# Two-layer diffusion trunk in fp32: the second gate's buffer placed elsewhere, the last grouped head's gate product and low part on VectorE, its context sums in a score bank

## The chip, the cores and the metric

The kernel runs on one core of a Trainium2 chip. The metric is the device time of one execution in microseconds (us). The engines are named as in the profile: PE (TensorE), DVE (VectorE), ACT (ScalarE), POOL (GpSimd), SP (SyncE, which issues nearly all DMAs here). Everything is float32. A matrix product in this precision is done as three fp32r matmuls: each operand is split into a high part (a cast to fp32r) and a low part (the rest), and high x high, low x high and high x low are added up in one PSUM bank.

## What is computed

Two layers of a trunk with two attention branches. Layer 0 has 512 latent and 256 context tokens (768 in all), layer 1 only the 512 latent ones are carried on. Per layer, cut to what matters:

```
hx, hc = adaLN-modulated RMSNorm of x (512 x 1024) and ctx (256 x 1024)
px = hx @ w_in                     # q, k, v of both branches, gate paths a_z, b_z, merge gates g_a, g_b
a_att = neighbourhood attention    # 8 heads of 64, 8 x 16 windows, also reads all context keys
b_att = grouped-query attention    # 8 query heads of 64, 2 key/value heads, reads all 768 keys
o_a = (a_att * silu(a_z)) @ w_o_a
o_b = (b_att * silu(b_z)) @ w_o_b
x   = x + gate_x * ((sigmoid(g_a) * o_a + sigmoid(g_b) * o_b) @ w_out)
# layer 0 does the same for the context tokens, which read context keys only
```

Layer 0 is called L0 below, layer 1 L1 (line numbers are written L352 and so on, with three or four digits).

## The kernel before

The program is one long Python function per layer, and a scheduler that simulates a timeline decides in which order each engine gets its instructions. Each engine then works its own list strictly in that order and waits on semaphores.

The grouped attention of a layer (`pipeline` with `gq_first` and `gq_values`) goes through the eight heads with one head of lag: the scores of head h, then the values of head h-1. In between PE gets filler work, here the product with `w_o_a` (tiles `gah`, `gal` for the high and low part of branch a's gated result, PSUM tile `psf`, written with `evac_a`, L593). A head's values are made in six steps. In each, PE transposes four 128x128 blocks of probabilities into a `pst` bank (L670), ACT casts them to the high part `pth` (L673), DVE subtracts for the low part `ptl` (L674), and PE multiplies both with the values into a `psv` bank (L973, L974). There are two `pst` banks. After the sixth step `head_out` adds the two halves of `psv` (ACT copy L682, DVE add L683, both in the single tile `ho`) and multiplies the sum into the gated tile `zb` (POOL, L684); the next copy into `ho` waits until that product has been read. In L0 each head also has context queries: one more step, whose sums have 256 columns and go to the same `psv` bank (`ctx_values`, L747 and L748), and a second `head_out`.

Before the last head's values, `early` allocates the buffers of the next stage and fills three quarters of `gated["b"]`. This is the split of `zb` into `gbh` (ACT cast, L558) and `gbl` (POOL subtraction, L559) by `hilo`, one instruction each per quarter f. The last quarter, f=3, needs the last two heads and is split after the pipeline. Then comes the product with `w_o_b` in four chunks (`o_chunks`), evacuated by `evac_b` (DVE L1008 and L1009, ACT L1011, DVE L1012) against the merge gate tiles `tg`. `load_tg` (L562) brings one from DRAM; `tg[1]` serves output columns f=0 to 3, `tg[3]` columns f=4 to 7. The filler product with `w_o_b`, once branch a's is done, goes to `psf`; after the pipeline five banks named `psx` are opened over those that the scores (`pss`, two of two banks each) and values (`psv`, one) had.

`big(name)` hands out large SBUF buffers from one pool in rotation. A tile that gets a buffer waits until the last reader of the tile that had it before is done. By the buffers of the program before, in L0 `tg[3]` lies where the queries `qb` were, `gbh` where the staged keys `gk` were and `gbl` where `gal` was. In L1 the three lie behind `qb`, `gal` and `gah`.

Of the kernel before, what the change touches and what calls it, by code (L numbers as in the profile page):

```python
# [12 lines left out]
ALU = mybir.AluOpType  # L13
# [55 lines left out]
def hybrid_kernel(es: ExitStack, tc, x, ctx, cvec, w_ada, w_ada0, small, gvec, w_in, w_o_a, w_o_b, w_out,  # L69
# [421 lines left out]
    def layer(l, hx, nxt, mid):  # L491
# [60 lines left out]
        def hilo_tiles(name):  # L552
            return [big(name + part).rearrange("p (f n) -> p f n", f=4) for part in "hl"]

        def hilo(src, dst, fs):
            sv = src.rearrange("p (f n) -> p f n", f=4)
            for f in fs:
                S.copy(R(dst[0][:, f, :ntok]), sv[:, f, :ntok])  # L558
                G.tensor_tensor(R(dst[1][:, f, :ntok]), sv[:, f, :ntok], dst[0][:, f, :ntok], ALU.subtract)  # L559

        def load_tg(c):
            nc.sync.dma_start(tg[c].rearrange("p (f n) -> p f n", f=4)[:, :, :ntok], gs[c][:, :, :ntok])  # L562
# [88 lines left out]
        if True:  # L651
# [25 lines left out]
            def head_out(po, e, dst):  # L677

                n = dst.shape[-1]
                m, o = 64 * e, 64 * (1 - e)  # L680
                t1 = att["p"].tile([128, 512], F32, tag="ho", name=nm("ho"), bufs=1)
                S.copy(t1[m:m + 64, :n], po[o:o + 64, :n])  # L682
                V.tensor_tensor(t1[m:m + 64, :n], po[m:m + 64, :n], t1[m:m + 64, :n], ALU.add)  # L683
                G.tensor_tensor(dst, dst, t1[m:m + 64, :n], ALU.mult)  # L684

            def rows(a, half):
                return a[64 * half:64 * half + 64]
# [53 lines left out]
            def ctx_values(p, vsl, dst, e):  # L741
                hi, lo = transpose_split(
                    [(p[:, 256 * i + 128 * k:256 * i + 128 * k + 128], 256 * k + 128 * i)
                     for k in range(2) for i in range(2)])
                po = psw(256, "v")
                for k in range(2):
                    T.matmul(po, vsl(4 + k), hi[:, 256 * k:256 * k + 256], start=k == 0, stop=False)  # L747
                    T.matmul(po, vsl(4 + k), lo[:, 256 * k:256 * k + 256], start=False, stop=k == 1)  # L748
                head_out(po, e, dst)
# [88 lines left out]
            def pipeline(fill, spread, scores_of, values_of, last=None, bg=[]):  # L838

                n = len(fill)  # L840
                prev = None
                for h in range(8):
                    att["bg"] = bg if h > 3 or pm["n"] == 1 else []
                    st = scores_of(h)
                    if prev is not None:
                        values_of(h - 1, prev)
                    run(fill, len(fill) - (n - n * min(h + 1, spread) // spread))
                    prev = st
                if last is not None:
                    run(fill, len(fill))  # L850
                    last()
                run(bg, len(bg))
                values_of(7, prev)
                run(fill, len(fill))

            akt = [k_tile(e, True) for e in range(2)]

            def na_first(h):
                j, e = h // 2, h % 2
# [124 lines left out]

            def early():

                for c in (1, 3):
                    tg[c] = big("tg")
                    load_tg(c)
                gated["b"] = hilo_tiles("gb")  # L990
                hilo(zb, gated["b"], range(3))
            bg = gate_steps((1,), att["p"]) if first else []
# [3 lines left out]
        with tc.tile_pool(name=f"mrg{l}", bufs=1, reuse_waits="tile") as mp:  # L996
            open_ps(x=5)
            extra = lambda name: mp.tile([128, 3072], F32, tag="extra", name=nm(name))
            gv = mp.tile([128, nv, DM], F32, tag="gate", name=nm("gate"), bufs=1)
            for v in range(nv):  # L1000
                src = gd[l][8 * v:8 * v + 8].rearrange("k p -> (k p)").unsqueeze(0)
                nc.sync.dma_start(gv[:, v, :], src.to_broadcast([128, DM]))
            hilo(zb, gated["b"], [3])
            mg = []

            def evac_b(f, n0, n1, ps):
                a, b = tg_part(0, f, n0, n1), tg_part(1, f, n0, n1)
                V.scalar_tensor_tensor(b, b, 1.0, ps, ALU.add, ALU.mult)  # L1008
                V.tensor_tensor(a, a, b, ALU.add)  # L1009
                hi, lo = [m[:, f % 4, n0:n1] for m in mg[f // 4]]  # L1010
                S.copy(R(hi), a)  # L1011
                V.tensor_tensor(R(lo), a, hi, ALU.subtract)  # L1012
            chunks = o_chunks("b", None, evac_b)
            chunks[0][0]()
            for i in range(4):
                if i < 3:
                    chunks[i + 1][0]()
                if i % 2 == 0:
                    mg.append(hilo_tiles("m"))
                for piece in chunks[i][1]:  # L1020
                    piece()

            nt = 6 if first else 4
            xv = [a.rearrange("p (t n) -> p t n", t=3) for a in (big("xt0"), extra("xt1"))]
            xts = []
            for t in range(nt):
                xt = xv[t // 3][:, t % 3, :]
                nc.sync.dma_start(xt, x_src(t) if first else xs1[128 * t:128 * t + 128, :])
                xts.append(xt)
            a_m = lambda part, k: mg[k // 4][part][:, k % 4, :]  # L1030
            bg = ada_steps(1, range(16), (1,), 2, mp) + [lambda: ada_mod(1)] if first else []
            run(bg, 1)
            per_bg = -(-len(bg) // nt)
            for n in range(2):
                w = load_w(w_out[l], 512 * n, 512, KT, mix_lo)

                def evac_o(t, ps, n=n, c=(0, 512)):
                    cs = slice(512 * n + c[0], 512 * n + c[1])
                    t1 = mp.tile([128, 512], F32, tag="t1", name=nm("t1"), bufs=2)[:, :c[1] - c[0]]
                    V.tensor_tensor(t1, ps, gv[:, 0 if t < 4 else 1, cs], ALU.mult)  # L1040
                    xt = xts[t]
                    V.tensor_tensor(xt[:, cs], xt[:, cs], t1, ALU.add)
                    if not first:
                        nc.sync.dma_start(o_lat[16 * t:16 * t + 16][:, :, cs], xt[:, cs])
                    elif n == 1:
                        if t < 4:
                            nc.sync.dma_start(xs1[128 * t:128 * t + 128, :], xt)
                        late.append(lambda: make_hx(1, t, xt, nxt(), mp))
                late = []
                for t in range(nt):  # L1050
                    if not first and n == 1 and t == nt - 1:
                        for c in ((0, 256), (256, 512)):
                            ps = psw(256)
                            tok_mm(ps, [[a[:, c[0]:c[1]] for a in x] for x in w], 256, a_m, t, 0, KT)
                            evac_o(t, ps, c=c)
                        break
                    tok_proj(w, 512, a_m, t, evac_o)
                    run(bg, per_bg)
                    run(late, len(late) - 1)
                run(late, len(late))  # L1060
# [186 lines left out]
```

## Time and profile before

| what | value |
|---|---|
| runs | 1146.18, 1144.71, 1144.48 us; median 1144.71 |
| profiled execution | 1144.91 us, of which 1143.1 us span from the first to the last instruction |
| granted PE clock | 0.999 |
| instructions | 17425, of which PE 6128 matmuls and as many weight loads |
| DMA | 135.08 MB, mean 118 GB/s |

The profiled execution is 0.20 us above the median. PE is busy nearly throughout: of the 40 slices of the span its row shows 9 tenths or more in all but the first and the last. The stages that the change touches are the ends of the grouped attention, at about 490 to 575 us (L0) and 1027 to 1090 us (L1). A row of the timeline reads: start, duration, engine, line, operation, tile written, tiles read, sizes, and in brackets the engine's idle time just before with the instruction that ended it.

### The profile page before, as it was taken

What the parts mean: (1) busy time and instruction counts of PE and PEld (TensorE: products, weight loads), DVE (VectorE), ACT (ScalarE), POOL (GpSimd) and SP (SyncE); (2) the same over time, 40 slices, a digit from 0 to 9 for tenths busy, and PEclk for the clock granted to TensorE, in tenths of its full rate; (3) what the DMA queues carried; (4) which work ended last, traced back from release to release, by engine and by line L of the source; (5) the groups of instructions that cost most, each with busy time, mean ns of one, the idle gap of its engine ahead of it and who ended that gap; (6) DMA issues with size and microseconds to landing.
All of it is one profiled execution on the core that took longest, in us unless ns stands there. A gap on an engine that the chain in (4) does not pass through costs nothing.

```text
span 1143.1 us, 17425 instructions
## 1 busy us (share of the span) xinstructions
PE 1120.7 (98%) x6128; PEld 947.6 (83%) x6128; DVE 816.3 (71%) x1535; ACT 581.4 (51%) x1185; POOL 480.6 (42%) x449
## 2 busy tenths in 40 slices
PE   7999999999999999999999999999999999999998
PEld 5788888888988888888788787888887888887787
DVE  6777688887554786697588655469777665898573
ACT  6553366665443565666330355337666355766521
POOL 1073354553364333453511226345453664465311
PEclk9999999999999999999999999999999999999999
DMA  9645212333323232451434424633332333152133
GB/s 368 241 123 157 85 56 70 99 116 97 118 94 97 96 101 86 98 217 38 152 124 134 148 69 122 186 103 116 99 114 65 111 103 102 65 175 92 64 126 97
DMA packets 91886, 135.08 MB, mean 118 GB/s; under 512 B 10804, under 2 KB 55064, under 8 KB 91160
## 3 DMA queue, kind: packets, MB, share of 16 engines
q1 hardware_dynamic: 91520, 133.87, 36.9%
q8 instruction: 48, 0.79, 0.3%
q14 instruction: 38, 0.31, 0.1%
q10 hardware_dynamic: 280, 0.12, 0.0%
HBM read 116.63 MB, written 17.32 MB: 117 GB/s over the span
## 4 chain that ended last, share of the span: by engine, by line
PE 87%; DVE 5%; DMA 2%; ACT 2%; issue 2%; POOL 1%; SPq 0%; ACTq 0%; POOLq 0%; DVEq 0%
PE psx L352 12%; PE psx L354 12%; PE psx L353 12%; PE psf L352 10%; PE psf L353 10%; PE psf L354 10%; PE pst L670 5%; PE pss L792 3%; PE pss L719 2%; PE pss L720 2%; PE psv L974 2%; PE psv L973 1%; PE pst L432 1%; DVE ptl L674 1%; DMA rawb<-in_w_ada_dram 1%
## 5 line engine op out<-in xcount | busy, mean ns | idle before, releaser
L674 DVE TENSOR_TENSOR ptl<-pst,pth 128x512 fp32r<-128x512 f32 (+1 forms) x176 | 115.9, 671 | 43.4 <-ACT pth L673 42.4
L673 ACT CAST pth<-pst 128x512 fp32r<-128x512 f32 (+1 forms) x176 | 99.2, 577 | 93.2 <-PE pst L670 53.1
L352 PE MATMUL psf<-hx,whi 128*128 128x512 f32 (+1 forms) x368 | 140.1, 381 | 0.1
L339 POOL TENSOR_TENSOR wlo<-raw,whi 128x512 fp32r<-128x512 f32 x68 | 95.9, 1414 | 103.5 <-ACT whi L337 86.2
L353 PE MATMUL psf<-hx,whi 128*128 128x512 f32 (+1 forms) x368 | 138.0, 375 | 0.0
L354 PE MATMUL psf<-hx,wlo 128*128 128x512 f32 (+1 forms) x368 | 137.6, 374 | 0.0
L352 PE MATMUL psx<-whi,hx 128*128 128x512 f32 (+1 forms) x368 | 137.6, 375 | 0.0
L354 PE MATMUL psx<-whi,hx 128*128 128x512 f32 (+1 forms) x368 | 135.8, 369 | 0.0
L353 PE MATMUL psx<-wlo,hx 128*128 128x512 f32 (+1 forms) x368 | 135.7, 369 | 0.0
L337 ACT CAST whi<-raw 128x512 fp32r<-128x512 f32 x136 | 82.8, 620 | 51.3 <-DMA raw<-in_w_in_dram 32.5
L322 ACT CAST whi<-raw 128x512 fp32r<-128x512 f32 x88 | 53.9, 622 | 100.5 <-PE psx L354 38.3
L670 PE MATMUL pst<-ident,p 128*128 128x128 f32 x640 | 99.5, 272 | 1.4 <-DVE ptl L674 0.9
L325 POOL TENSOR_TENSOR wlo<-raw,whi 128x512 fp32r<-128x512 f32 x36 | 49.5, 1378 | 119.6 <-ACT whi L322 106.2
L339 DVE TENSOR_TENSOR wlo<-raw,whi 128x512 fp32r<-128x512 f32 x68 | 68.0, 1001 | 32.1 <-ACT whi L337 31.6
L670 PEld LDWEIGHTS pst<-ident,p 128*128 128x128 f32 x640 | 77.8, 141 | 13.4 <-DVE ptl L674 1.3
L660 POOL TENSOR_TENSOR p<-p,r 128x512 f32<-128x512 f32 (+1 forms) x64 | 83.5, 1305 | 4.9
L659 POOL TENSOR_SCALAR r<-r 128x1 f32<-128x1 f32 x64 | 22.2, 347 | 150.4 <-DVE r L654 126.9
L352 PEld LDWEIGHTS psx<-whi,hx 128*128 128x128 f32 x368 | 69.5, 189 | 12.3 <-issue 0.8
L354 PEld LDWEIGHTS psx<-whi,hx 128*128 128x128 f32 x368 | 69.4, 189 | 11.9
L354 PEld LDWEIGHTS psf<-hx,wlo 128*128 128x128 f32 x368 | 69.3, 188 | 11.7
L353 PEld LDWEIGHTS psx<-wlo,hx 128*128 128x128 f32 x368 | 69.5, 189 | 10.7
L352 PEld LDWEIGHTS psf<-hx,whi 128*128 128x128 f32 x368 | 69.4, 189 | 10.5 <-ACT zt L517 0.3
(253 smaller groups left out, 3049.7 us busy)
## 6 DMA issues: line engine op xcount, KB each, us to landing
raw<-in_w_in_dram SPq DMA_DIRECT2D x168, 256.0 KB, 2.9
rawb<-in_w_ada_dram SPq DMA_DIRECT2D x64, 256.0 KB, 2.8
gs<-zt SPq DMA_DIRECT2D x32, 256.0 KB, 2.0
raw<-in_w_out_dram SPq DMA_DIRECT2D x32, 256.0 KB, 2.9
tg<-gs SPq DMA_DIRECT2D x4, 1536.0 KB, 6.8
rawx<-in_w_ada_dram SPq DMA_DIRECT2D x8, 512.0 KB, 7.7
raw<-in_w_o_a_dram SPq DMA_DIRECT2D x16, 256.0 KB, 2.7
raw<-in_w_o_b_dram SPq DMA_DIRECT2D x16, 256.0 KB, 3.3
```

The costliest lines, as they stand in the source:

```text
L322: S.copy(hi[:, :n], raw[:, :n])
L325: e.tensor_tensor(lo[:, :n], raw[:, :n], F(hi[:, :n]), ALU.subtract)
L337: S.copy(hi, raw)
L339: lo_eng(i).tensor_tensor(lo, raw, F(hi), ALU.subtract)
L352: T.matmul(ps, lhs[0], rhs[0], start=first, stop=False)
L353: T.matmul(ps, lhs[0], rhs[1], start=False, stop=False)
L354: T.matmul(ps, lhs[1], rhs[0], start=False, stop=last)
L660: G.tensor_tensor(p[:, c0:c1], p[:, c0:c1], r[:, i:i + 1].to_broadcast([128, c1 - c0]), ALU.mult)
L670: T.transpose(pt[:, c0:c0 + 128], src, ident)
L673: S.copy(hi[:, n0:n1], pt[:, n0:n1])
L674: V.tensor_tensor(lo[:, n0:n1], pt[:, n0:n1], F(hi[:, n0:n1]), ALU.subtract)
L792: T.matmul(pss.rearrange("p (a b n) -> p a b n", a=2, b=2), qi, blocks_of(k, *at), start=b, stop=not b)
```

## The change

It has four parts. `tg[3]` is no longer allocated and loaded in `early`, but in the loop over the chunks of `o_b`, behind the load of the second chunk's weights. So `gbh` and `gbl` move up one place in the rotation. In L0 `gbh` now lies behind `qb`, `gbl` behind `gk` and `tg[3]` behind `gal`; in L1 they lie behind `qb`, `gal` and `gah`. A flag `att["end"]` is set before the values of the last grouped head: with it `head_out` multiplies on DVE instead of POOL, and `ctx_values` takes its bank from the scores (`"s"`) instead of the values (`"v"`). The split of the last quarter f=3 is done span by span (512 columns, in L0 also 256), its low part on DVE.

```diff
-        def hilo(src, dst, fs):
+        def hilo(src, dst, fs, parts=None, lo=G):
             sv = src.rearrange("p (f n) -> p f n", f=4)
             for f in fs:
-                S.copy(R(dst[0][:, f, :ntok]), sv[:, f, :ntok])
-                G.tensor_tensor(R(dst[1][:, f, :ntok]), sv[:, f, :ntok], dst[0][:, f, :ntok], ALU.subtract)
+                for a, b in parts or [(0, ntok)]:
+                    S.copy(R(dst[0][:, f, a:b]), sv[:, f, a:b])
+                    lo.tensor_tensor(R(dst[1][:, f, a:b]), sv[:, f, a:b], dst[0][:, f, a:b], ALU.subtract)
...
-                G.tensor_tensor(dst, dst, t1[m:m + 64, :n], ALU.mult)
+                (V if att["end"] else G).tensor_tensor(dst, dst, t1[m:m + 64, :n], ALU.mult)
...
-                po = psw(256, "v")
+                po = psw(256, "s" if att["end"] else "v")
...
                 run(bg, len(bg))
+                att["end"] = last is not None
                 values_of(7, prev)
...
-                for c in (1, 3):
-                    tg[c] = big("tg")
-                    load_tg(c)
+                tg[1] = big("tg")
+                load_tg(1)
                 gated["b"] = hilo_tiles("gb")
                 hilo(zb, gated["b"], range(3))
...
-            hilo(zb, gated["b"], [3])
+            hilo(zb, gated["b"], [3], spans, V)
...
             for i in range(4):
                 if i < 3:
                     chunks[i + 1][0]()
+                if i == 0:
+                    tg[3] = big("tg")
+                    load_tg(3)
```

How the order moves, at three places. In the rows below, numbers behind a name tell tiles apart.

The end of L0's last head on PE, before: `psf` is the first product with `w_o_b`, `psv_6333` the head's values, `psv_6413` its context sums and `psx_6479` the first tile of the next stage.

```order
L670 MATMUL pst_6404<-ident,p_6155 128x128 x4
L974 MATMUL psv_6333<-ptl_6395,vb_3516 128x512
L353 MATMUL psf_6462<-gbl_6326,whi_6438 128x512
L354 MATMUL psf_6462<-gbh_6325,wlo_6440 128x512
L352 MATMUL psf_6462<-gbh_6325,whi_6444 128x512
L353 MATMUL psf_6462<-gbl_6326,whi_6444 128x512
L354 MATMUL psf_6462<-gbh_6325,wlo_6446 128x512
L747 MATMUL psv_6413<-pth_6409,vb_3516 128x256
L748 MATMUL psv_6413<-ptl_6410,vb_3516 128x256
```

And the same place in the changed program.

```order
L353 MATMUL psf_6464<-gbl_6324,whi_6444 128x512
L354 MATMUL psf_6464<-gbh_6323,wlo_6446 128x512
L976 MATMUL psv_6331<-pth_6381,vb_3516 128x512
L977 MATMUL psv_6331<-ptl_6382,vb_3516 128x512
L976 MATMUL psv_6331<-pth_6392,vb_3516 128x512
L671 MATMUL pst_6402<-ident,p_6155 128x128 x4
L977 MATMUL psv_6331<-ptl_6393,vb_3516 128x512
L748 MATMUL pss_6411<-pth_6407,vb_3516 128x256
L749 MATMUL pss_6411<-ptl_6408,vb_3516 128x256
```

All nine matmuls of `psf` with quarters f=0 to 2 now stand in a row ahead of the head's last values (before, they were spread over these, the last five behind the transposes of the context step), so nothing stands between the last transposes and the context sums, which go to a `pss` bank. Behind the context sums `psx` begins in both programs. Its first tile lies in the bank of `pss_6411` now and waits for the DVE sum that reads that; before, its first tile lay in a free score bank, and the second one, in the bank of `psv_6413`, waited for that sum.

The same stretch of L0 on DVE, before:

```order
L674 TENSOR_TENSOR ptl_6410<-pst_6404,pth_6409 128x512
L683 TENSOR_TENSOR ho_6400<-psv_6333,ho_6400 64x512
L683 TENSOR_TENSOR ho_6418<-psv_6413,ho_6418 64x256
L1008 SCALAR_TENSOR_TENSOR tg_6321<-tg_6321,psf_6462 128x512
L1008 SCALAR_TENSOR_TENSOR tg_6321<-tg_6321,psx_6479 128x256
```

And changed:

```order
L675 TENSOR_TENSOR ptl_6408<-pst_6402,pth_6407 128x512
L684 TENSOR_TENSOR ho_6398<-psv_6331,ho_6398 64x512
L685 TENSOR_TENSOR zb_4170<-zb_4170,ho_6398 64x512
L684 TENSOR_TENSOR ho_6416<-pss_6411,ho_6416 64x256
L685 TENSOR_TENSOR zb_4170<-zb_4170,ho_6416 64x256
L560 TENSOR_TENSOR gbl_6324<-zb_4170,gbh_6323 128x512
L560 TENSOR_TENSOR gbl_6324<-zb_4170,gbh_6323 128x256
```

The two products `zb` and the low part of f=3 have come over from POOL. On POOL the low parts of f=0 to 2 have moved up as well: two of them from behind the last product with `gal` to right behind a `zb` of the sixth head, ahead of a softmax division `p`, the third behind that division.

L1 on PE, before, where five of the six matmuls of `psf` that use f=0 and 1 stand (the sixth, `gbh` x `whi`, stands some twelve rows ahead of them):

```order
L670 MATMUL pst_11528<-ident,p_11300 128x128
L353 MATMUL psf_11871<-gbl_11754,whi_11847 128x512
L354 MATMUL psf_11871<-gbh_11753,wlo_11849 128x512
L352 MATMUL psf_11871<-gbh_11753,whi_11847 128x512
L973 MATMUL psv_11472<-pth_11522,vb_9709 128x512
L353 MATMUL psf_11871<-gbl_11754,whi_11847 128x512
L354 MATMUL psf_11871<-gbh_11753,wlo_11849 128x512
L974 MATMUL psv_11472<-ptl_11523,vb_9709 128x512
```

And changed:

```order
L352 MATMUL psf_11873<-gbh_11753,whi_11847 128x512
L353 MATMUL psf_11873<-gbl_11754,whi_11847 128x512
L354 MATMUL psf_11873<-gbh_11753,wlo_11849 128x512
L352 MATMUL psf_11873<-gbh_11753,whi_11847 128x512
L976 MATMUL psv_11474<-pth_11502,vb_9711 128x512
L353 MATMUL psf_11873<-gbl_11754,whi_11847 128x512
L354 MATMUL psf_11873<-gbh_11753,wlo_11849 128x512
L977 MATMUL psv_11474<-ptl_11503,vb_9711 128x512
```

The five have moved up two steps of the head's values, to the wait for `ptl_11503` (`ptl_11501` before). Around this place in L1, POOL now has the two low parts ahead of a weight's low part `wlo` and a division `p`, and DVE has a `wlo` ahead of the score maximum `mx` instead of behind it.

The DMA of `tg[3]` moves on SP's queue from among the weights of `w_o_b` to behind the first weight of `w_out`; behind it now stand further weights of `w_out`, the gate `gv` and the residual tiles.

More of the change, by code (lines that the diff above doesn't have):

```diff
@@ L856, in layer @@
             akt = [k_tile(e, True) for e in range(2)]
+            att["end"], att["turn"] = False, 0
             def na_first(h):
```

## The prediction, made before the changed kernel ran

> **What bounds the kernel now.** I read the page's busy times first, then the chain that ended last, then the waits in the two stretches that the change touches, then the timelines of PE, ACT, DVE and POOL there. On the page:
>
> ```profile
> PE 1120.7 (98%) x6128; PEld 947.6 (83%) x6128; DVE 816.3 (71%) x1535; ACT 581.4 (51%) x1185; POOL 480.6 (42%) x449
> PE 87%; DVE 5%; DMA 2%; ACT 2%; issue 2%; POOL 1%; SPq 0%; ACTq 0%; POOLq 0%; DVEq 0%
> tg<-gs SPq DMA_DIRECT2D x4, 1536.0 KB, 6.8
> ```
>
> PE is busy for 1120.7 of 1143.1 us and is 87% of the chain. The change takes no matmul away. So all it can win is the 22.4 us in which PE does nothing, start and end of the program included, and of these only the waits that it touches. A faster DVE, ACT or POOL gains nothing except where PE waits for it. The longest two waits of L0's stretch, 549 to 561 us, are not PE's own (total, count, longest):
>
> ```profile
> POOL gbl L559 <- PE psf L353: 3.6, 1, 3.6
> ACT ho L682 <- POOL zb L684: 3.1, 1, 3.1
> ```
>
> `gbl` could not start before PE had read its buffer for the last time, and the copy `ho` waited for the product `zb`, which stood behind it on POOL. PE's timeline shows, in brackets, what came of both: 0.79 us of idle time put down to `gbl` and 1.21 us put down to the DVE add `ho`.
>
> ```profile
> 552.43 0.48 PE L352 MATMUL psf<-gbh,whi 128*128 128x512 f32 x1
> ...
> 554.43 0.60 PE L670 MATMUL pst<-ident,p 128*128 128x128 f32 x4
> 554.78 0.48 PE L974 MATMUL psv<-ptl,vb 128*128 128x512 f32 x1
> 555.10 0.40 PE L353 MATMUL psf<-gbl,whi 128*128 128x512 f32 x1
> ...
> 555.57 0.40 PE L352 MATMUL psf<-gbh,whi 128*128 128x512 f32 x1
> 556.75 0.50 PE L353 MATMUL psf<-gbl,whi 128*128 128x512 f32 x1 [0.79 <-POOL gbl L559]
> ...
> 557.79 0.28 PE L352 MATMUL psx<-gbh,whi 128*128 128x256 f32 x1
> ...
> 558.74 0.28 PE L354 MATMUL psx<-gbh,wlo 128*128 128x256 f32 x1
> 560.22 0.50 PE L352 MATMUL psx<-gbh,whi 128*128 128x512 f32 x1 [1.21 <-DVE ho L683]
> ```
>
> Starts give the pace: 0.23 us for a matmul of 512 columns (two steps from 555.10 to 555.57), 0.32 behind transposes (554.78 to 555.10), 0.35 for four transposes (554.43 to 554.78), and 0.12 for 256 columns (557.79 to 558.74 are eight steps). By that pace 556.75 is 0.95 late and 560.22 is 1.36 late: 2.3 us of stall in L0. The other engines:
>
> ```profile
> 555.07 0.59 ACT L673 CAST pth<-pst 128x512 fp32r<-128x512 f32 x1 [1.76 <-PE pst L670]
> 555.68 0.58 ACT L682 COPY ho<-psv 64x512 f32<-64x512 f32 x1
> 559.34 0.36 ACT L682 COPY ho<-psv 64x256 f32<-64x256 f32 x1 [3.09 <-POOL zb L684]
> ...
> 551.43 1.78 DVE L339 TENSOR_TENSOR wlo<-raw,whi 128x512 fp32r<-128x512 f32 x1
> 555.69 0.69 DVE L674 TENSOR_TENSOR ptl<-pst,pth 128x512 fp32r<-128x512 f32 x1 [1.28 <-ACT pth L673]
> 556.41 0.69 DVE L683 TENSOR_TENSOR ho<-psv,ho 64x512 f32<-64x512 f32 x1
> 559.74 0.43 DVE L683 TENSOR_TENSOR ho<-psv,ho 64x256 f32<-64x256 f32 x1 [2.64 <-ACT ho L682]
> 568.10 0.68 DVE L325 TENSOR_TENSOR wlo<-raw,whi 128x512 fp32r<-128x512 f32 x1
> 574.13 0.42 DVE L1008 SCALAR_TENSOR_TENSOR tg<-tg,psx 128x256 f32<-128x256 f32 x1
> ...
> 550.82 5.87 POOL L559 TENSOR_TENSOR gbl<-zb,gbh 128x768 fp32r<-128x768 f32 x3 [3.60 <-PE psf L353]
> 558.03 1.28 POOL L684 TENSOR_TENSOR zb<-zb,ho 64x512 f32<-64x512 f32 x1
> ```
>
> **L0, step by step.** The low parts of f=0 to 2 move up on POOL to right behind the sixth head's `zb`, when PE has done the last scores that read `gk`; `gbl` then waits for nothing that PE is about to use, and the 0.95 goes. PE runs its nine `psf` matmuls from 552.43 without a stop (0.32 and eight times 0.23, to 554.59), then three value matmuls (to 555.28), then the context step's transposes. The cast `pth` starts 0.64 behind them (555.07 against 554.43), at 555.92; `ptl` 0.62 behind that (555.69 against 555.07), at 556.54; the 512-column `ho` add 0.72 later (556.41 against 555.69), at 557.26, done 557.95.
>
> Now `zb` on DVE. No row shows it. The nearest are the add of the same shape, 0.69, and a DVE subtraction with both inputs in SBUF, 0.68 at 568.10 and 1.78 at 551.43. In the second POOL had begun its first `gbl` (1.9 of 5.87) 0.6 us before, and 551.43 + 1.78 is some 0.5 us behind that one's end: DVE was held until POOL had finished an instruction. I take 0.68, because in the new order POOL has nothing of the old cluster left at this time; 1.78 is the upper end. So `zb` ends at 558.65, the 256-column copy starts at 558.68, the add 0.40 later (559.74 against 559.34), at 559.08, and PE follows 0.48 after that (560.22 against 559.74), at 559.56.
>
> The catch is which matmul that is. Before, the nine 256-column matmuls of the first `psx` ran ahead of the wait, in a free score bank. Now they are the ones that wait, since the context sums lie in the bank that they get. They take 1.07 us (0.95 for eight steps, and 0.12), so the 512-column `psx` starts at 560.63 instead of 560.22: **L0 loses 0.4 us**. The 2.3 us of old stall go, but PE now waits where work used to lie between the context step's transposes and its values (about 0.6 for `pth` and 0.6 for `ptl`) and some 1.9 us in front of `psx` (`ptl` is done at 557.23, and the last of the four context matmuls starts 0.4 later). Bounds: -2.3 (no wait left) and +1.5 (with 1.1 more for `zb`).
>
> The Trainium skill, page "SBUF — State Buffer", section "Who interferes with whom", has a rule against this part: a DVE instruction with two SBUF inputs shares a read port with POOL, and whichever starts first holds it for its whole instruction. The row with 1.78 agrees. By that rule alone, with any POOL work in front of `zb`, the sum for L0 would be +1.5 instead of +0.4.
>
> The low part of f=3 on DVE (0.69 by the same row) and `zb` with 256 columns follow behind the add, from 559.5 on, and end by about 561.5, casts included; PE has `psx` matmuls of f=0 to 2 before it, 1.07 and nine at 0.23, to 562.7. That cover makes them free; without it the 1.1 us of two DVE instructions would be PE's. The `tg[3]` DMA now waits for the last product with `gal`, the same event that released `gbl` at 550.82, and takes 6.8: it lands near 557.6. Its first reader comes behind the evacuations of f=3, the last of which is at 574.13. That is 16 us of cover. What stands around it on SP's queue:
>
> ```profile
> 538.65 19.65 SPq L320 DMA_DIRECT2D raw<-in_w_out_dram  x3
> ```
>
> These three weights went out over 538.65 to 558.30, one by one as buffers came free; a `tg[3]` at 550.8 stands behind the first of them and holds the other two up only until a moment at which the queue was still waiting for buffers. I put the move at 0, with 0.3 either way.
>
> **L1.** PE, then DVE, then POOL:
>
> ```profile
> 1053.34 0.48 PE L352 MATMUL psf<-gbh,whi 128*128 128x512 f32 x1
> ...
> 1055.62 0.50 PE L974 MATMUL psv<-ptl,vb 128*128 128x512 f32 x1 [1.54 <-DVE ptl L674]
> 1057.21 0.48 PE L353 MATMUL psf<-gbl,whi 128*128 128x512 f32 x1
> 1058.93 0.60 PE L670 MATMUL pst<-ident,p 128*128 128x128 f32 x4
> 1060.93 0.65 PE L670 MATMUL pst<-ident,p 128*128 128x128 f32 x4 [0.43 <-DVE ptl L674]
> 1074.70 0.50 PE L974 MATMUL psv<-ptl,vb 128*128 128x512 f32 x1 [0.23 <-DVE ptl L674]
> ...
> 1052.34 0.95 DVE L956 TENSOR_REDUCE mx<-pss 128x1 f32<-128x768 f32 x1
> 1053.21 1.75 DVE L339 TENSOR_TENSOR wlo<-raw,whi 128x512 fp32r<-128x512 f32 x1
> 1054.88 1.27 DVE L674 TENSOR_TENSOR ptl<-pst,pth 128x512 fp32r<-128x512 f32 x2
> ...
> 1051.56 1.42 POOL L339 TENSOR_TENSOR wlo<-raw,whi 128x512 fp32r<-128x512 f32 x1 [0.30 <-PE pst L670]
> 1054.38 2.95 POOL L559 TENSOR_TENSOR gbl<-zb,gbh 128x512 fp32r<-128x512 f32 x2
> ```
>
> PE waits 1.54 us for a `ptl` that DVE starts at 1054.88, because `wlo` in front of it ended only at 1054.96 (1.75 in place of 0.68), 0.58 behind the moment at which POOL went over from one instruction to the next, 1054.38: it was held by what POOL did before. In the new order `wlo` starts in the slot of `mx`, at 1052.34, is held only until POOL's first `gbl` ends (about 1052.7, an estimate: half of 2.95 from 1051.26, when POOL was idle), and `mx` follows it; `ptl` starts near 1054.05, 0.8 earlier. Meanwhile PE has the five `psf` matmuls to do, 1.15 us at 0.23, so the matmul with `ptl` starts at about 1055.05, 0.6 earlier than 1055.62. The five are then missing in 1057.21 to 1058.47, where only `ptl` binds, so the transposes at 1058.93 come 1.1 us earlier. From there to 1074.70 the two `pst` banks set the pace (the wait at 1060.93 is such a one): transposes, cast, subtraction, in a loop that PE cannot speed up. What reached it early stays early: **L1 gains 1.1 us**. Bounds: 0, if the loop is bound by something else ahead of it, and -1.8, the two waits 1.54 and 0.23 whole. POOL's `p` behind the two low parts comes 2.5 us later; it belongs to the eighth head, and the transposes at 1058.93 are still the seventh's, so that costs nothing. At L1's end the products on DVE touch a stretch in which PE has the `psx` matmuls of f=0 to 2 to do, without a wait: 0.
>
> The casts `gbh`, moved up by tens of us on ACT, cost nothing if they slip between casts that PE needs; the slow rival is about that. All other shifts of order lie where PE's timeline shows no wait: 0, with 0.3 either way.
>
> **Sum.** +0.4 - 1.1 = -0.7 against the profiled execution, 1144.91, which is 0.2 above the median shown: **1144.2 us**. Its own bounds: from -2.3 - 1.8 to +1.5 + 0, so 1140.8 to 1146.4; a measurement of this kernel cannot tell changes under about 0.2%, or 2.3 us.
>
> **Rivals.** *All stalls go.* If the bank of the context sums came free before PE gets to `psx`, or the first `psx` got another bank, L0 would gain its 2.3 and L1 up to 1.8: 1140.8. For it: the nine `psf` matmuls in a row give DVE a free field. Against it: 1.9 us separate the last context matmul from the add that frees the bank, and nothing in PE's order fills them.
>
> *The low part in L1 stays late.* `gbl` still lies behind `gal` there, whose last reader on PE stands right ahead of that of `gah`. If it then comes no earlier than before, PE's five moved matmuls wait for it, L1 gains nothing and only L0's loss is left: 1145.3.
>
> *DVE held by POOL.* If a POOL weight split starts just ahead of `zb`, the 1.1 us of the bounds come on top: 1145.3 again with L1's gain, decided by whether POOL is at work at about 558. That is the rule of the Trainium skill's page above ("SBUF — State Buffer", "Who interferes with whom") at this place.
>
> *Slower: a cast blocks ACT.* In L0 the cast of `gbh` for f=1 now stands right ahead of two `pth` casts and waits for a `zb` of POOL:
>
> ```profile
> 497.80 0.84 POOL L684 TENSOR_TENSOR zb<-zb,ho 64x256 f32<-64x256 f32 x1 [1.81 <-DVE ho L683]
> 498.24 1.07 ACT L673 CAST pth<-pst 128x512 fp32r<-128x512 f32 x2 [3.69 <-PE psv L973]
> 500.29 1.28 DVE L674 TENSOR_TENSOR ptl<-pst,pth 128x512 fp32r<-128x512 f32 x2
> ```
>
> `zb` ends at 498.64 and the cast takes some 0.8 (half again the 0.54 of a 512-column one in 498.24's row), so the first `pth` is done at 500.0, 0.3 before DVE takes it; what slack PE has beyond that I do not count. If `zb` slips behind two more POOL instructions of 1.28, the casts come 2.6 late and PE loses 2.3; the same at one cast of L1 makes 4.6, and with the sum 1148.8. It decides from 0.3 us of slip. Against it: POOL was idle for 1.81 us ahead of this `zb`, waiting for DVE.
>
> **How the numbers follow.** My forecast 0.58; all stalls go 0.13; L1's low part late 0.12; DVE held 0.09; ACT blocked 0.08. Faster by over 0.2% (below 1142.4) takes the first rival and a tail of 0.05 of the forecast, 0.18 in all; slower (above 1147.0) is the ACT case, 0.08; within 0.2% is the rest, 0.74. The range goes up to the sum's own upper bound and down to where most of L0's and L1's stalls would be won together; it leaves out the end of the first rival and the last one, less than 0.2: 1141.7 to 1146.4.
>
> **What would show it.** In the changed profile: no wait of `psf` on `gbl` in L0; POOL's first `gbl` long before 549; a wait of about 1.9 us in front of the first `psx`, put down to DVE's `ho`; `zb` on DVE at 0.68; in L1 the wait of 1.54 gone and the last `psv` about 1.1 us closer to the start of the `gbh` matmuls. I am wrong if `psx` does not wait, if POOL's or DVE's rows there are longer than here, or if PE shows a new wait on `pth` near 501 or 1036.

## The result, and the profile after

The changed kernel takes 1154.22 us (median of 4 runs, 1153.03 to 1154.86) against 1144.96 (1144.48 to 1146.18): 1.0076 times the time before, 95% interval 1.0064 to 1.0089. That is 9.3 us slower; forecast was 1144.2, with 1141.7 to 1146.4 as range. The profiled execution took 1153.03 with a span of 1151.1, 8.0 more than before.

Of PE's waits over the whole span (total us, count, longest), one line stands out in the changed kernel:

```profile
PE psf L352 <- DVE tg L594: 5.5, 4, 3.8
```

and the same line before:

```profile
PE psf L352 <- DVE tg L593: 0.9, 2, 0.7
```

`tg` on DVE is the evacuation of a `psf` bank. One wait of 3.8 us for it is new, and a second is 0.79. The long one is in L1, where I had forecast a gain. PE, DVE and POOL there, from the timeline of the changed kernel (start, duration, engine; in brackets the idle time before):

```profile
1056.13 0.60 PE L671 MATMUL pst<-ident,p 128*128 128x128 f32 x4
1060.57 0.50 PE L352 MATMUL psf<-gbh,whi 128*128 128x512 f32 x1 [3.84 <-DVE tg L594]
...
1082.98 0.39 PE L352 MATMUL psx<-gbh,whi 128*128 128x512 f32 x1
...
1054.25 5.67 DVE L658 TENSOR_SCALAR p<-p,r 128x768 f32<-128x768 f32 x1
1059.84 0.68 DVE L594 SCALAR_TENSOR_TENSOR tg<-tg,psf 128x512 f32<-128x512 f32 x1
1060.43 0.68 DVE L339 TENSOR_TENSOR wlo<-raw,whi 128x512 fp32r<-128x512 f32 x1
...
1054.16 0.20 POOL L660 TENSOR_SCALAR r<-r 128x1 f32<-128x1 f32 x1
1054.33 2.52 POOL L560 TENSOR_TENSOR gbl<-zb,gbh 128x512 fp32r<-128x512 f32 x2
1056.82 1.26 POOL L339 TENSOR_TENSOR wlo<-raw,whi 128x512 fp32r<-128x512 f32 x1
1058.04 1.46 POOL L661 TENSOR_TENSOR p<-p,r 128x768 f32<-128x768 f32 x1
```

The same engines before, at the same work:

```profile
1052.99 0.60 PE L670 MATMUL pst<-ident,p 128*128 128x128 f32 x4
...
1075.04 0.40 PE L352 MATMUL psx<-gbh,whi 128*128 128x512 f32 x1
...
1051.21 0.62 DVE L657 TENSOR_SCALAR p<-p,r 128x768 f32<-128x768 f32 x1
...
1051.06 0.20 POOL L659 TENSOR_SCALAR r<-r 128x1 f32<-128x1 f32 x1
1051.56 1.42 POOL L339 TENSOR_TENSOR wlo<-raw,whi 128x512 fp32r<-128x512 f32 x1 [0.30 <-PE pst L670]
1052.95 1.46 POOL L660 TENSOR_TENSOR p<-p,r 128x768 f32<-128x768 f32 x1
```

DVE's softmax division `p` takes 0.62 us before and 5.67 after. Read the rows of POOL under it: before, POOL paused 0.30 us from 1051.26, and the division ran then. After, the two low parts `gbl` close that pause; POOL works without one from 1054.16 to 1059.50, and DVE's division ends at 1059.92, 0.42 behind the end of POOL's last instruction. Behind the division on DVE stands `tg`, which frees the bank that PE's next product needs: PE stands still for 3.84 us.

The same happens to a smaller degree in L0:

```profile
532.29 2.32 DVE L658 TENSOR_SCALAR p<-p,r 128x256 f32<-128x256 f32 x2
534.65 0.69 DVE L594 SCALAR_TENSOR_TENSOR tg<-tg,psf 128x512 f32<-128x512 f32 x1
...
530.37 4.10 POOL L560 TENSOR_TENSOR gbl<-zb,gbh 128x768 fp32r<-128x768 f32 x2
...
535.39 0.39 PE L352 MATMUL psf<-gah,whi 128*128 128x256 f32 x1 [0.79 <-DVE tg L594]
...
553.37 0.48 PE L352 MATMUL psf<-gbh,whi 128*128 128x512 f32 x1
557.50 0.39 PE L748 MATMUL pss<-pth,vb 128*128 128x256 f32 x1 [0.45 <-ACT pth L674]
558.23 0.38 PE L749 MATMUL pss<-ptl,vb 128*128 128x256 f32 x1 [0.34 <-DVE ptl L675]
560.59 0.58 PE L352 MATMUL psx<-gbh,whi 128*128 128x256 f32 x1 [1.74 <-DVE ho L684]
560.97 0.41 PE L353 MATMUL psx<-gbl,whi 128*128 128x256 f32 x1
561.19 0.41 PE L354 MATMUL psx<-gbh,wlo 128*128 128x256 f32 x1
...
563.11 0.60 PE L352 MATMUL psx<-gbh,whi 128*128 128x512 f32 x1
...
558.94 0.69 DVE L685 TENSOR_TENSOR zb<-zb,ho 64x512 f32<-64x512 f32 x1
```

Of the two small divisions, the first gets in between POOL's two `gbl`; the second is held until the second `gbl` ends at 534.47, and PE waits 0.79 at 535.39. At the end of L0's last head the chain is the one forecast: no wait for `gbl`, `zb` at 0.69 on DVE, then waits of 0.45, 0.34 and 1.74. But the matmuls behind it go at 0.22 us a step for 256 columns (560.97 to 561.19) instead of 0.12. The windows show why (PE, PEld, DVE, ACT and POOL busy, then the granted clock, the DMA share and GB/s); the row of before stands in the second fence:

```profile
556.00:560.00 4.00, 2.07 (x11) 1.25 (x9) 2.08 (x3) 1.45 (x3) 0.00 (x0) 1.00 0.80 311
560.00:564.00 4.00, 3.41 (x13) 3.14 (x14) 1.88 (x4) 1.10 (x3) 0.00 (x0) 0.57 0.98 353
...
1060.00:1064.00 4.00, 3.43 (x11) 2.38 (x12) 3.18 (x5) 0.00 (x0) 0.00 (x0) 0.74 0.42 126
1064.00:1068.00 4.00, 3.61 (x18) 2.58 (x17) 1.84 (x4) 2.64 (x5) 1.26 (x2) 0.84 0.34 104
```

```profile
560.00:564.00 4.00, 3.78 (x21) 3.31 (x22) 0.17 (x1) 1.46 (x2) 2.69 (x3) 1.00 0.94 277
```

After PE's pause the granted clock is 0.57 in one stretch and 0.74 and 0.84 in the other; before, it was 1.00.

The ledger, each number a difference of two starts of the same matmul, after less before: first `psf` with `gbh` in L0 +0.94 (553.37 against 552.43); the 512-column `psx` behind it +2.89 (563.11 against 560.22); the transposes in L1 +3.14 (1056.13 against 1052.99); first `psf` with `gbh` in L1 +7.23 (1060.57 against 1053.34); first `psx` in L1 +7.94 (1082.98 against 1075.04). So 0.9 comes from the hold in L0, 2.0 to 2.2 from the end of L0's last head, 4.1 from the hold in L1, and 0.7 net behind it, where the clock was low and the old stalls of L1 are gone. By the two pages, PE's idle time explains 3.6 of the 8.0 us (22.4 before, 26.0 after); the rest is busy time, 1125.1 against 1120.7 for the same 6128 matmuls, with two stretches of 3.4 us at half the clock in it.

### The profile page after: what moved, and what is told of

Its sections match the earlier page's. It is cut to its first block, busy times and chain, and to the rows that moved or that the text cites. A ratio compares the mean times of both kernels' runs of the same rounds, so it can differ in the third digit from the quotient of the medians.

```text
span 1151.1 us, 17426 instructions
## 1 busy us (share of the span) xinstructions
PE 1125.1 (98%) x6128; PEld 951.5 (83%) x6128; DVE 828.2 (72%) x1541; ACT 582.7 (51%) x1186; POOL 473.8 (41%) x444
## 4 chain that ended last, share of the span: by engine, by line
PE 87%; DVE 6%; DMA 3%; issue 2%; ACT 2%; POOL 1%; SPq 0%; ACTq 0%; DVEq 0%; POOLq 0%
PE psx L352 12%; PE psx L354 12%; PE psx L353 12%; PE psf L352 10%; PE psf L353 10%; PE psf L354 10%; PE pst L671 5%; PE pss L793 2%; PE pss L720 2%; PE pss L721 2%; PE psv L977 2%; PE psv L976 2%; PE pst L432 1%; DVE ptl L675 1%; DMA rawb<-in_w_ada_dram 1%
## 5 line engine op out<-in xcount | busy, mean ns | idle before, releaser
L658 DVE TENSOR_SCALAR p<-p,r 128x512 f32<-128x512 f32 (+2 forms) x96 | 77.7, 823 | 2.4
```

The source lines that it names most:

```text
L658: V.tensor_scalar(p[:, c0:c1], p[:, c0:c1], r[:, i:i + 1], 0.5, ALU.mult, ALU.mult)
```

## The experiments

Theory A: the moved low parts `gbl` leave POOL no pause, DVE cannot start its division, and the wait for `tg` follows; the buffers' move carries the loss. The rival: the tail of L0's last head carries most of it, with PE's waits at the score bank and the low clock behind them. Ratios are against the kernel before.

**Buffers alone** (`tg[3]` loaded later; the tail as before):

```diff
-                for c in (1, 3):
-                    tg[c] = big("tg")
-                    load_tg(c)
+                tg[1] = big("tg")
+                load_tg(1)
...
+                if i == 0:
+                    tg[3] = big("tg")
+                    load_tg(3)
```

> Only the buffer part of the change: tg[3] allocated and loaded later, so gbh and gbl move up; head_out, the last low part and the context sums as before. Theory A (a softmax division on DVE is shut out while POOL works off the moved low parts without a pause; the evacuation behind it comes late, PE waits, and after a long wait the granted clock drops): in L1 a DVE division of 5 to 6 us near 1054, PE idle 3 to 4 us in front of the first psf of branch b, a clock under 1.0 behind it; in L0 about 0.9 lost near 535; the end of L0's last head within 1 us of before. Sum 5 to 7 us over before, 1150 to 1152. Theory B (the work that the change puts on DVE at the end of a head is what delays DVE): within 1 us of before, 1144 to 1146.

Measured: 1152.33 us, 1.0065 (1.005 to 1.008). The timeline has the division held again, over the same run of POOL:

```profile
1052.52 5.68 DVE L657 TENSOR_SCALAR p<-p,r 128x768 f32<-128x768 f32 x1
```

PE waits 3.85 for `tg` at 1058.86. The move of the buffers alone makes 7.4 of the 9.3 us.

**The tail alone** (product and low part on DVE, context sums in a score bank; buffers as before), run twice, the second time for one more profile:

```diff
-                G.tensor_tensor(dst, dst, t1[m:m + 64, :n], ALU.mult)
+                (V if att["end"] else G).tensor_tensor(dst, dst, t1[m:m + 64, :n], ALU.mult)
...
-                po = psw(256, "v")
+                po = psw(256, "s" if att["end"] else "v")
...
-            hilo(zb, gated["b"], [3])
+            hilo(zb, gated["b"], [3], spans, V)
```

> Only the other parts: the last grouped head's products and its last low part on DVE, its context sums in a score bank; buffers as before. Theory A: L1 within 0.5 us of before, no division over 2 us; L0 loses 1 to 3 us at its last head, with a wait in front of the first psx of over 1.5 us and a clock drop behind it. Sum 1145.5 to 1148. Theory B: L1 loses 4 to 5 us also here, 1149 to 1152.

> The same program as the run with only the DVE parts and the score bank, for one more profile. Its runs spread over 2.6 us. If the clock drop behind the 1.9 us wait in L0 comes in some executions and not in others, this profile may show it: clock under 0.8 at 560 to 564 with a time of 1147.5 or more, or 1.0 with 1146 or less. A mixture of these (drop with the low time, or none with the high) would speak against it.

Measured: 1146.9 us (10 runs, 1145.65 to 1148.24), 1.0017 (1.0007 to 1.0026); the second time 1146.1 in its one run. 1.9 and the 7.4 of the buffers add up to the whole. In both profiles PE waits 1.9 us in front of `psx` and the clock stays at 1.00 behind it; here the first:

```profile
560.00:564.00 4.00, 4.00 (x25) 3.55 (x25) 1.03 (x2) 0.41 (x1) 0.00 (x0) 1.00 0.81 268
```

But the ten times fall in two groups: four of 1145.65 to 1146.07 with a mean granted clock of 0.999 to 1.000 over the span, six of 1146.8 to 1148.24 with 0.998. The groups' means lie 1.8 us apart; 0.001 to 0.002 of the clock is worth 1.1 to 2.3 over 1145 us. So the drop seems to come in some executions of one program and not in others; neither profile caught it. The next experiment has what the traces show about when it comes.

**A fuller wait.** In the changed kernel, eight matmuls whose result nobody reads fill PE's wait in front of the first `psx` of L0 and of no other place:

```diff
+                if att["end"]:
+                    idle = psw(512, "t")
+                    for k in range(8):
+                        T.matmul(idle, vsl(4), lo, start=k == 0, stop=k == 7)
```

> The changed kernel with matmuls in front of the first psx of L0 that nothing reads: eight of 512 columns into a transpose bank, behind the context sums of the last head (one in L1's last head does not exist, so L0 only). If the clock drop follows PE's idle time: PE works through the 1.7 us, the granted clock stays 1.0 at 560 to 564, and L0 ends 1.0 to 1.4 us earlier than in the changed kernel although PE does more; L1 as changed; 1152 to 1154. If the drop comes from the DMA traffic that begins at the same time (tg[3] and weights), the clock is 0.5 to 0.7 there all the same and nothing is gained.

Measured: 1152.96 us, 1.0068 (1.0054 to 1.0082), by the ratios some 0.9 us below the changed kernel; the intervals of the two ratios overlap, so the rows have to decide. PE and the clock:

```profile
558.68 2.01 PE L753 MATMUL pst<-ptl,vb 128*128 128x512 f32 x8
560.59 0.39 PE L352 MATMUL psx<-gbh,whi 128*128 128x256 f32 x1
...
561.98 0.40 PE L352 MATMUL psx<-gbh,whi 128*128 128x512 f32 x1
...
560.00:564.00 4.00, 4.00 (x22) 3.27 (x22) 1.88 (x4) 1.10 (x3) 0.00 (x0) 1.00 0.96 345
```

`psx` begins at the same 560.59, with DMA at 0.96 against 0.98; only PE's idleness is gone, and the clock stays at 1.00, so the DMA alone does not lower it. The 512-column `psx` comes at 561.98 instead of 563.11: the low clock costs 1.13 us there.

When the clock falls can be read from the traces. They hold the moments at which the granted clock changed. In all 14, each change lies a whole number of stretches of 3.413 us behind the first rise of the same trace, and that rise comes at another time in each, from 7.76 to 10.59 us. On this grid the clock fell behind every stretch at full clock in which PE was idle for 1.87 us or more (ten up to PE's last matmul), and behind none with 1.75 or less. Two stretches of the changed kernel, then two of the tail alone (its first profile):

```profile
556.72:560.13 3.41, 1.35 (x7) 0.63 (x5) 2.10 (x4) 1.55 (x4) 0.00 (x0) 1.00 0.76 290
560.13:563.55 3.42, 2.96 (x12) 2.77 (x13) 1.86 (x4) 1.00 (x2) 0.00 (x0) 0.50 0.99 350
```

```profile
555.41:558.82 3.41, 1.91 (x9) 1.04 (x8) 2.74 (x3) 1.06 (x3) 2.67 (x2) 1.00 0.01 4
558.82:562.24 3.42, 2.65 (x16) 2.39 (x17) 1.88 (x4) 1.28 (x3) 0.00 (x0) 1.00 0.70 244
```

In the first, PE is idle for 2.06 of 3.41 us, and the next stretch has 0.50. In the second, the grid divides PE's wait of 1.9 us: 1.50 idle, then 0.77, and the clock stays. Laid at every place over the rows of the tail alone, the grid finds a stretch with that much idle time in 0.57 (bound 1.87) to 0.64 (bound 1.75) of the places, an estimate; six of its ten times are in the slower group. It also limits what the filled wait shows by itself: at that run's place of the grid (556.22 to 559.64) the changed kernel's own rows hold only 1.57 us of idle time, so its clock might have stayed at 1.00 there unfilled. With the wait filled, no place of the grid finds more than 0.78 us.

**Context sums back in a value bank**, the rest as changed:

```diff
-                po = psw(256, "s" if att["end"] else "v")
+                po = psw(256, "v")
```

> The changed kernel with the context sums of the last head back in the value bank. Theory A: nine matmuls of the first psx run ahead of the wait for ho, the wait is under 1.2 us and the clock stays at 1.0 behind it; L0 gains 1.5 to 2.5 us on the changed kernel, L1 as changed: 1151.5 to 1153. If the clock drop does not hang on the length of the wait, L0 gains only 0.2 to 0.6.

Measured: 1154.2 us, 1.0081 (1.0065 to 1.0098): no gain, an expectation missed. The wait has only moved ahead of the context sums, which now need the bank that `ho` empties:

```profile
PE psv L748 <- DVE ho L684: 1.9, 1, 1.9
```

The clock behind it is 0.59 at 560 to 564. The bank's choice decides which matmul waits, not whether.

**The early low parts on DVE**, the rest as changed, so that POOL gets its pause:

```diff
-                hilo(zb, gated["b"], range(3))
+                hilo(zb, gated["b"], range(3), lo=V)
```

> The changed kernel with the early low parts (f=0 to 2) of branch b on DVE instead of POOL. Theory A: without the low parts POOL makes no long run; the division in L1 takes under 1.5 us, PE's wait of 3.8 us and the clock drop behind it are gone, L0's 0.9 near 535 too; the end of L0's last head stays as changed. 5 to 6 us faster than the changed kernel: 1147 to 1149. Theory B (DVE has too much to do there): more DVE work makes it slower still, over 1154.

Measured: 1150.95 us, 1.0052 (1.0037 to 1.0067): better by 3.3, but not to the 1147 to 1149 expected. POOL still has three instructions in a row, and now DVE's own `gbl` are held:

```profile
1055.27 3.97 DVE L560 TENSOR_TENSOR gbl<-zb,gbh 128x512 fp32r<-128x512 f32 x2
...
1055.30 0.70 POOL L660 TENSOR_SCALAR r<-r 128x1 f32<-128x1 f32 x1
1055.97 1.29 POOL L339 TENSOR_TENSOR wlo<-raw,whi 128x512 fp32r<-128x512 f32 x1
1057.23 1.46 POOL L661 TENSOR_TENSOR p<-p,r 128x768 f32<-128x768 f32 x1
```

The first `gbl` began 0.03 us ahead of POOL's `r`, and `r` took 0.70 instead of 0.20; the second came only after POOL's `p`. A hold is seen on both sides, and who has it is read from whose row is too long. PE waits 2.31.

**Divisions on POOL.** All softmax divisions of L1's last head go to POOL, the rest as changed:

```diff
-                    softmax_tail(p, 768, r[:, 0:1], [(0, 768)], G if i in GQ_POOL else None)
+                    softmax_tail(p, 768, r[:, 0:1], [(0, 768)], G if i in GQ_POOL or att["h"] == 7 and not first else None)
```

> The changed kernel with all four divisions of the last grouped head of L1 on POOL (before, two of four were on DVE). Theory A (a DVE instruction that needs the port shared with POOL is shut out while POOL works without a pause): the evacuation of psf no longer stands behind a division, so PE's wait for tg in L1 (3.8 us) goes; but the next DVE instruction with two SBUF inputs, a weight's low part wlo, comes behind it and can be held in the same way, then ptl is late by up to 5 us. L1 loses 0 to 5 us, and the long DVE instruction of the stretch, if there is one, is a wlo. L0 as changed. 1148 to 1154. Theory C (the evacuation is late since PE's last gah matmuls come late, whatever DVE does): PE's wait for tg stays at 3 to 4 us.

Measured: 1153.79 us (1148.99 to 1155.07), 1.0061 (1.004 to 1.0081). `tg` is free now, but the next DVE instruction with its operands in SBUF, a weight's low part, takes the hold, for longer:

```profile
1056.17 6.62 DVE L339 TENSOR_TENSOR wlo<-raw,whi 128x512 fp32r<-128x512 f32 x1
```

It ends 0.55 behind POOL's last instruction (1062.24), and PE waits 4.9 for the `ptl` that stands behind it. One held instruction moved off DVE is not enough: every one in the stretch has to go.

**Both off DVE.** L0 as before; in L1 the buffers as changed, the divisions on POOL as above, and with them the low parts of `w_o_b`:

```diff
-                    st["w"] = load_w2(src, 256 * i, 4, mix_lo)
+                    st["w"] = load_w2(src, 256 * i, 4, pool_lo if br == "b" and not first else mix_lo)
```

> L0 as before. L1 with the new place of the buffers alone (no products on DVE), the divisions of its last grouped head on POOL, and the low parts of w_o_b's weights in L1 on POOL: in the stretch at 1050 to 1060 DVE has no instruction left that needs the shared port. Theory A: no DVE instruction over 1.3 us there, no wait of PE over 1 us, the clock at 1.0, and the 1.1 us that the blind prediction saw in L1 appear: 1143.4 to 1144.6, between 0.5 us slower and 1.5 faster than before. If the loss in L1 has another cause, 1148 or more.

The same without the second edit, so that `wlo` alternates between POOL and DVE:

> As the faster version of the last batch (L0 as before; in L1 the buffers' new place and the divisions of the last grouped head on POOL), but the low parts of w_o_b's weights alternate between POOL and DVE as before. The stretch then has one DVE instruction left that shares POOL's port, a wlo near 1053, in front of a ptl that PE waits for. Theory A: that wlo takes 5 to 7 us, PE waits 4 to 5 us for ptl, 1148 to 1151. If only the division mattered, it is as fast as the version without it: 1143 to 1144.5.

And both edits with the buffers as before:

> The kernel before, buffers as before, with only the two edits that take the sharing instructions off DVE in L1: the last grouped head's divisions and the low parts of w_o_b's weights on POOL. It tells how much of the faster version's 1.7 us comes from the buffers. Old wait of 1.5 us for ptl at 1054: gone in any case, since the wlo that was held there is on POOL. If the buffers' new place is worth the 1.1 us of the blind prediction: 1144.0 to 1145.0, behind the faster version by about 1. If it is worth nothing: 1143 to 1144.

Measured: 1143.63 (11 runs, 0.9985, 0.9976 to 0.9993), 1150.71 (1.0046, 1.0031 to 1.0062) and 1143.31 (11 runs, 0.9982, 0.9974 to 0.9991). With nothing left on DVE in that stretch that POOL can hold, L1's new buffers cost nothing that these runs resolve, and do not bring the 1.1 us: 1143.63 with them, 1143.31 without, and from the first `psf` with `gbh` to the first `psx` 20.75 us with them, 20.37 without (21.70 in the kernel before). The wait of 1.54 in the kernel before, which I wanted to fill, was itself the held `wlo`: with `wlo` on POOL it is 0.22 in the kernel with the buffers as before:

```profile
1053.69 0.50 PE L974 MATMUL psv<-ptl,vb 128*128 128x512 f32 x1 [0.22 <-DVE ptl L674]
```

The kernel between them took 1145.48 in its profiled execution and 1150.64 to 1150.85 in the three others. The profile shows the lucky one: `wlo` got in after POOL's two `gbl`, and POOL's `r` had to wait for it (0.65 instead of 0.20):

```profile
1052.45 2.34 DVE L339 TENSOR_TENSOR wlo<-raw,whi 128x512 fp32r<-128x512 f32 x1
...
1054.20 0.65 POOL L659 TENSOR_SCALAR r<-r 128x1 f32<-128x1 f32 x1
```

The others are 5.2 us longer, at a mean clock of 0.996 against 1.000; that `wlo` was held to the end there, as where the divisions alone were moved, is argued from that, not seen.

**The gate's product on DVE by itself**, on top of the best two: `zb` of the last head, in both layers with the new buffers of L1, in L0 only with the buffers as before.

```diff
-                G.tensor_tensor(dst, dst, t1[m:m + 64, :n], ALU.mult)
+                (V if att["end"] else G).tensor_tensor(dst, dst, t1[m:m + 64, :n], ALU.mult)
```

> The faster version, and the last grouped head's products zb on DVE (context sums in the value bank, last low part on POOL as before). In L0, zb with 512 columns is ready at 557.1, while POOL works off three low parts and a weight split without a pause until about 558.0. Theory A: zb is held until then and takes about 1.4 us, ending 558.5; the copy and the add behind it come 0.8 earlier than with POOL's zb at 558.03 to 559.31, so the second psx starts 0.6 to 0.9 earlier: 1142.4 to 1143.2. Without any hold it would be 1.3 earlier: 1142.2 or less.

> The version without the buffers' move (divisions and weight splits of L1's end on POOL) with the last head's products zb of L0 on DVE. The two gains lie 500 us apart and should add: L1 about 2 us by the profile of the one, L0 about 0.7 by the profile of the other (zb again held to about 1.35 by POOL). Span 2.5 to 3 us under that of before; timed 1142.3 to 1143.0. If the 0.7 of L0 does not appear in the time, 1143.1 to 1143.6.

Measured: 1143.39 (11 runs, 0.9984, 0.9975 to 0.9992) and 1142.71 (9 runs, 0.9976, 0.9966 to 0.9986). The context sums stay in the value bank here, and the nine 256-column `psx` run ahead of the wait. The last one's rows:

```profile
557.42 1.36 DVE L684 TENSOR_TENSOR zb<-zb,ho 64x512 f32<-64x512 f32 x1
...
556.94 1.29 POOL L339 TENSOR_TENSOR wlo<-raw,whi 128x512 fp32r<-128x512 f32 x1
...
559.75 0.50 PE L352 MATMUL psx<-gbh,whi 128*128 128x512 f32 x1 [0.42 <-DVE ho L683]
```

`zb` is held by POOL's `wlo` for half of its 1.36 us, and still PE's wait of 1.21 shrinks to 0.42 (0.43 in the other one). In the times the gain is not resolved: the kernel with the new buffers misses its expected 1142.4 to 1143.2 and has the ratio that it had without this edit (0.9984 against 0.9985), and the intervals of the other pair overlap. This last kernel, 2.4 us faster than the one before, is the best of those run.

## Why the prediction was wrong

**The step that failed** is the one in L1: "`wlo` ... is held only until POOL's first `gbl` ends", and with it "POOL's `p` behind the two low parts ... costs nothing". A hold ends where DVE gets in between two instructions of POOL, and it need not get in at the first: it was shut out over four in a row (5.67 us). Getting in at the first is what nearly all held rows here show (the counts are in the last section), so the step had rows behind it; but the whole L1 term hung on it, and I gave its failure no price. I had the row that showed a hold, 1.75, and the order that puts `gbl`, `wlo` and `p` on POOL behind each other, and read neither as a run without a pause. I also costed `wlo` as the first DVE instruction concerned; the division and `tg` stand ahead of it. The term: -1.1 forecast; +4.1 at the wait and +4.8 up to the first `psx`.

**"All other shifts of order ... 0 with 0.3 either way"** failed in L0 too, at 530 to 535, by a hold of a single instruction: +0.94 where I had looked at no row of POOL.

**The gain itself** was misread. The 1.54 us was no lack of work for PE but a held instruction; without the hold the five moved matmuls bring no gain that shows (1143.63 against 1143.31).

**L0's last head.** The chain was right: no wait on `gbl`, `zb` on DVE at 0.69 (forecast 0.68), waits of 0.45, 0.34 and 1.74 (forecast 0.6, 0.6, 1.9). In the kernel with the filled wait, 8.61 us lie between the first `psf` with `gbh` and the 512-column `psx`, 7.79 before; one `psf` matmul of f=3 now stands among the nine `psx`, 0.32 (1.39 us from 560.59 to 561.98, 1.07 without it). That leaves +0.50 for a forecast of +0.41. What failed is the price of a wait: I took PE to resume at full pace, and in this execution the clock cost 1.13 on top.

**The rivals.** "DVE held by POOL" was the right mechanism with a wrong place and price: `zb` in L0, +1.1 and a chance of 0.09, where `zb` was not held at all (POOL was idle from 556 to 564, by the two rows of the windows). The Trainium skill, page "SBUF — State Buffer", section "Who interferes with whom", says of two instructions that want the port pair which VectorE shares with GpSimd that the first holds it for its whole instruction and the other fully blocks. The trace agrees on who is held: `p`, `wlo`, `gbl` and `zb`, all with their inputs in SBUF, and not `ptl` with one input in PSUM (0.69 us at 1052.53 amid POOL's run in the kernel with both edits). On how long, "its whole instruction" is too little here: 5.67 us are more than any one instruction of POOL in that stretch (1.46 at most). The rival of the ACT cast did not come: no wait of PE on `pth` near 501 or 1036.

**What stays open.** What decides whether DVE gets in at a handover between two POOL instructions. It did in the kernel before, and in the profiled execution of the alternating one at the second handover. It did not at one place of L1 in the six other traced kernels with the new buffers that leave DVE an instruction to hold there. That the clock falls by PE's idle time in a stretch of the grid is read off the traces of these kernels; no run was made to find the bound between 1.75 and 1.87 us.

## What to carry to other kernels

Before moving work to POOL or forward on it, look on its timeline for the pauses, and ask which DVE instruction with all inputs in SBUF runs in each: if the move closes the pause, that instruction and all behind it on DVE wait for at least one instruction of POOL, and can wait until POOL stops, here up to 6.6 us. In a stretch where POOL must work through, put such work on POOL too and leave DVE those with an operand in PSUM; that alone was worth 1.8 us here, where the change cost 9.3. And a wait of PE that looks like missing work should first be followed to the instruction behind which its releaser stood, and that row compared with the same form elsewhere (1.75 against 0.68): filling the wait with other work leaves the cause in place.

## What the runs showed of the hardware

- A DVE instruction with its operands in SBUF can be passed over at several handovers of POOL: 5.67 and 5.68 us over four POOL instructions, 6.62 over a chain of six, 3.97 for two with one of them let in. It is the exception: of 504 `wlo` on DVE in the 14 traces that took over 1.0 us, all but two (6.62 and 2.34) took 1.96 or less. At 330 handovers (POOL's next instruction within 0.06 us, those to or from `r` left out) with a `wlo`, `p` or `gbl` running on DVE, DVE was passed over at 17, all at one place of L1 (1052 to 1061), in seven kernels with the new buffers. The loser at a handover shows in its row: 0.65 to 0.70 us for an `r` of 0.20 on POOL.
- Who gets in differs between executions of one program: 1145.48 and 1150.64 to 1150.85 us.
- The granted clock changed only on a grid of 3.413 us, whose place differs between the traces; it fell to 0.50 behind each stretch in which PE was idle for 1.87 us or more, and behind none with 1.75 or less. A wait of 1.7 to 1.9 us can so be divided by the grid and cost nothing, or fall into one stretch and cost 1.13 us behind it; one of 3.84 us puts at least 1.92 into one stretch. The Trainium skill, page "TensorE: Matmul & The Clock Gate", in its table of the two states, puts the half rate behind at least one idle window of about 3.4 us. The length agrees with the grid here, but no wait of PE at the end of L0's last head was that long: over half a stretch of idle time was enough. The page also calls the window free-running; the first rise at 7.76 to 10.59 us agrees.
